# Finishing output rows: the final weight multiplied early on GpSimd, one half scaled on ScalarE, and a shorter root at the end

## The chip, the cores and the metric

The kernel runs on one core of a Trainium2 chip. The core has five engines with their own in-order instruction queues: TensorE (PE in the profile, with its weight loads as PEld), VectorE (DVE), ScalarE (ACT), GpSimd (POOL) and SyncE (SP), whose queue here only issues DMAs. The engines wait for each other through semaphores. The metric is the device time of one execution in microseconds (us), lower is better.

## The reference

The reference is one layer of a bidirectional encoder, applied to two sequences ("prompt" and "sample", 1024 tokens of 1024 features each, float32), followed by a final normalisation:

```python
def layer(x, c, ...):
    ...                                   # attention and Fourier mixing side by side
    x = x + ga1 * mix
    h2 = rmsnorm(x, g_ffn) * (1.0 + sc2) + sh2
    ffn = (jax.nn.silu(h2 @ w_gate) * (h2 @ w_up)) @ w_down
    return x + ga2 * ffn

def trunk(x, c):
    ...
    return rmsnorm(x, g_final)            # y = x / sqrt(mean(x*x) + 1e-6) * g_final, row by row
```

Only the last two lines matter here. For each output row the kernel needs `x + ga2 * ffn`, its mean of squares over 1024 features, the reciprocal root of that, and then the row times the root times the final weight `g_final`.

## The kernel before, in words

The two sequences run one after the other; `s` is 0 for the prompt and 1 for the sample. The work in front (conditioning vectors, attention, Fourier part) takes the first 750 us or so; then comes the feed-forward part of the prompt and then that of the sample, each with a gate/up stage and a down stage.

All large products are done to nearly float32 accuracy in three passes: `split` (lines 62 to 64) makes of a tile a rounded high part `wh` (a cast on ScalarE, line 63) and a remainder `wl` (a subtraction on VectorE, line 64), and `mm3` (lines 78 to 81) adds three matmuls. So every matmul operand loaded from memory costs a cast and a subtraction before TensorE can use it; there are eight buffers each for `wh` and `wl`.

The feed-forward matrices are multiplied by a scheme of Strassen's kind with seven products of half size. In the down stage `prod2` (one product) loops over `f`, 11 blocks: it loads two tiles with DMAs on SP (lines 1758 and 1759), splits them, and adds 12 matmuls into four PSUM banks, one for each group `t` of 128 rows. The products go into the bank sets X, Y and Z in a fixed order. After each block a `hook` may issue one step of other work; the steps are lists of small functions. `behind()` puts what a step issues on ScalarE and VectorE after the latest split. Beyond that, a compile-time planner decides the order of the instructions on each engine from its own estimate of when each is ready.

The output has four quarters: row half 0 or 1, and column half 0 or 1. `c11` and `u2` hold the two column halves of row half 0, `p1` and `u3` those of row half 1, each as four tiles of 128 x 512 (one for each `t`). `gf` holds the final weight, copied to all partitions.

- During the product into Z with index 4, the steps `early0` add the residual to `u2` and square-sum `c11`, which is complete.
- During the last product into Y (index 3), the steps `early1` complete `u3`, and `early2` square-sums `u3` on ScalarE (`first_squares`, with a tiny addition on POOL). In the sample, `early2` also multiplies `c11` by its half of `gf` on VectorE (line 1859).
- Then `rows_out` finishes row half 1: `last_part` completes the missing quarter (`p1`) on VectorE (lines 1788 and 139), square-sums it on ScalarE (line 1790), and calls `rstd`, a reciprocal root of six tiny POOL operations (lines 106 to 111: add, power, and a correction step of four). Two steps later `scale` multiplies both halves by root and weight in one VectorE operation each (line 1799), and one step later `store` writes both from SP (line 1805). In the prompt these steps run during the last product into Z (index 2); in the sample they run between the matmuls of the end.
- Row half 0 of the prompt is finished in the same way, but its steps are kept in `pending` and run in the first blocks of the sample's gate/up stage, behind splits.
- Row half 0 of the sample is the end of the kernel. The operands of the last product were split earlier and lie in SBUF (`held`), so it runs on TensorE row group by row group. After each group comes `last_part`, then a multiplication of `u2` by its weight (line 1878) and a scaling of `c11` and `u2` by the root on VectorE (line 1880), and two stores (line 1881).

Of the kernel before, what the change touches and what calls it, by code (L numbers as in the profile page):

```python
# [12 lines left out]
F32 = mybir.dt.float32  # L13
# [3 lines left out]
ALU = mybir.AluOpType  # L17
# [4 lines left out]
P = 128  # L22
# [31 lines left out]
def hybrid_encoder_kernel(ctx: ExitStack, tc: tile.TileContext, a: dict):  # L54
    nc = tc.nc
# [28 lines left out]
    tiny = ctx.enter_context(tc.tile_pool(name="tiny", bufs=4))  # L84
# [8 lines left out]
    mhalf = const.tile([P, 4], F32, name="mhalf")  # L93
# [3 lines left out]
    def rstd(ms, n, rest=None):  # L97

        v = tiny.tile([P, 4], F32, name="rs_v")[:, :n]
        y = tiny.tile([P, 4], F32, name="rs_y")[:, :n]  # L100
        w = tiny.tile([P, 4], F32, name="rs_w")[:, :n]
        r = tiny.tile([P, 4], F32, name="rs_r")[:, :n]
        if rest is None:
            nc.gpsimd.tensor_scalar(out=v, in0=ms, scalar1=EPS, scalar2=None, op0=ALU.add)
        else:
            nc.gpsimd.tensor_tensor(out=v, in0=ms, in1=rest, op=ALU.add)
        nc.gpsimd.tensor_tensor(out=y, in0=v, in1=mhalf[:, :n], op=ALU.pow)  # L107
        nc.gpsimd.tensor_tensor(out=w, in0=y, in1=y, op=ALU.mult)
        nc.gpsimd.tensor_tensor(out=w, in0=w, in1=v, op=ALU.mult)
        nc.gpsimd.tensor_scalar(out=w, in0=w, scalar1=-0.5, scalar2=1.5, op0=ALU.mult, op1=ALU.add)  # L110
        here["p"] = nc.gpsimd.tensor_tensor(out=r, in0=w, in1=y, op=ALU.mult).ins
        return r

    s1 = [const.tile([P, NC], F32, name=f"s1_{s}") for s in range(2)]
# [23 lines left out]
    def add(out, x, y, eng):  # L138
        eng.tensor_tensor(out=out, in0=x, in1=y, op=ALU.add)  # L139
# [27 lines left out]
    with ExitStack() as st:  # L167
        p1b = st.enter_context(ExitStack())
        w2 = p1b.enter_context(tc.tile_pool(name="p1b", bufs=1, side="right", reuse_waits="tile"))
        w = st.enter_context(tc.tile_pool(name="p1", bufs=1, reuse_waits="tile"))  # L170
        pp = st.enter_context(tc.tile_pool(name="p1_ps", bufs=8, space=PSUM, reuse_waits="tile"))

        def bank():
            return pp.tile([P, 512], F32, tag="b", name="bank")
# [281 lines left out]
        def zboth(k, between):  # L456
            eo = st1["eo", k]
            pz = [bank() for _ in range(2)]
            mz = tiny.tile([P, 4], F32, name="mz")
            if 3 < k + 2 < nk:  # L460
                norm(k + 2)
            for i in range(2):
                for c in range(NC):
                    mm3(pz[i][:, :DZ], eo[i][0][:, c, :], eo[i][1][:, c, :], wz_h[:, c, :], wz_l[:, c, :], c == 0, c == NC - 1)
                    if i == 0 and c in (1, NC - 1):
                        between(c)
            if k < 2 or k == nk - 1:
# [46 lines left out]
        def flush():  # L514
            for dst, t in st1.pop("st", ()):
                nc.sync.dma_start(dst, t)
# [288 lines left out]
        z = zboth(nk - 1, lambda c: flush() if c == 1 else None)  # L805
# [409 lines left out]
    with ExitStack() as st:  # L1215
        w = st.enter_context(tc.tile_pool(name="p3", bufs=1, side="right", reuse_waits="tile"))
# [118 lines left out]
        for k in range(nit + 4):  # L1335
# [7 lines left out]
            if k < nit:  # L1343
                s, b, h, u = items[k]
# [22 lines left out]
            m = k - 11  # L1367
# [7 lines left out]
    with ExitStack() as st:  # L1375
        w = st.enter_context(tc.tile_pool(name="p5", bufs=1, reuse_waits="tile"))
# [6 lines left out]
        def quad(tag, dt=F32):  # L1383
            return w.tile([P, 4, 512], dt, tag=tag, name=tag, bufs=1)
# [94 lines left out]
        r, wc = S.pop("rgu"), quad("H41")  # L1479
# [16 lines left out]
        r = wc = None  # L1496
# [27 lines left out]
        def val():  # L1524
            return w5.tile([P, 512], F32, tag="v", name="val", bufs=VALS)
# [10 lines left out]
        gf, first_w = None, None  # L1536
        order = [fi + half * (NF // 2) for fi in range(NF // 2) for half in range(2)]
        pending = []
        for s in range(2):
# [80 lines left out]
            for n, f in enumerate(order):  # L1620
# [51 lines left out]
                x, y, z = bank(), bank(), bank()  # L1672
# [5 lines left out]
                u2 = val()  # L1678
# [6 lines left out]
                u3 = val()  # L1685
# [18 lines left out]
            ga = w5.tile([P, D], F32, tag="ga", name="ga2", bufs=1)  # L1704
            if gf is None:
                gf = S["gf"]
# [69 lines left out]
            m, me = {}, {}  # L1776

            def first_squares(half, t, v):

                m[half, t] = tiny.tile([P, 2], F32, name=f"ms_{half}")  # L1780
                me[half, t] = tiny.tile([P, 1], F32, name=f"me_{half}")
                jk = val()
                nc.scalar.activation(jk, v, AF.Square, scale=1.0 / 32.0, accum_out=m[half, t][:, 0:1])
                nc.gpsimd.tensor_scalar(out=me[half, t], in0=m[half, t][:, 0:1], scalar1=EPS, scalar2=None, op0=ALU.add)

            def last_part(half, t, v, g, ps, z, m=m, me=me, ga=ga):

                nc.vector.tensor_tensor(out=z, in0=ps, in1=ga[:, 512 * g : 512 * g + 512], op=ALU.mult)  # L1788
                add(v, v, z, nc.vector)
                nc.scalar.activation(z, v, AF.Square, scale=1.0 / 32.0, accum_out=m[half, t][:, 1:2])  # L1790
                return rstd(m[half, t][:, 1:2], 1, me[half, t])

            def rows_out(v0, v1, half, g, ps, s=s, last_part=last_part):

                rr = {}

                def scale(t):
                    for j, v in enumerate((v0[t], v1[t])):
                        nc.vector.scalar_tensor_tensor(out=v, in0=v, scalar=rr[t][:, 0:1], in1=gf[:, 512 * j : 512 * j + 512],  # L1799
                                                       op0=ALU.mult, op1=ALU.mult)  # L1800

                def store(t):
                    r0 = 512 * half + P * t
                    for j, v in enumerate((v0[t], v1[t])):
                        nc.sync.dma_start(ys[s][r0 : r0 + P, 512 * j : 512 * j + 512], v)
                    v0[t] = v1[t] = None

                def at(i):
                    if 0 <= i - 3 < 4:
                        store(i - 3)  # L1810
                    if 0 <= i - 2 < 4:
                        scale(i - 2)
# [22 lines left out]
            u2 = [val() for _ in range(4)]  # L1835
# [3 lines left out]
            c11 = [val() for _ in range(4)]  # L1839
# [3 lines left out]
            u3 = [val() for _ in range(4)]  # L1843
            for t in range(4):
                add(u3[t], Y[t], p1[t], nc.vector)
            Z = [bank() for _ in range(4)]
# [8 lines left out]

            def early2(t):
                first_squares(1, t, u3[t])
                if s == 1:
                    nc.vector.tensor_tensor(out=c11[t], in0=c11[t], in1=gf[:, :512], op=ALU.mult)

            prod2(Z, 4, True, True, hooks([functools.partial(early0, t) for t in range(4)]
                                          + [functools.partial(resid, p1[t], t, (1, 0), None) for t in range(4)],
# [6 lines left out]
            if s == 1:  # L1869
                ext = quad("H20")  # L1870
                for t in range(4):
                    tt = slice(t * P, t * P + P)
                    for f, q in enumerate(held):
                        mm3(Z[t], q[:, 0, tt], q[:, 1, tt], q[:, 2, :], q[:, 3, :], False, f == NF // 2 - 1, True)
                        if steps and f % 3 == 2:
                            steps.pop(0)()
                    r = last_part(0, t, u2[t], 1, Z[t], ext[:, t, :])
                    nc.vector.tensor_tensor(out=u2[t], in0=u2[t], in1=gf[:, 512:], op=ALU.mult)
                    for g, v in enumerate((c11[t], u2[t])):
                        nc.vector.tensor_scalar(out=v, in0=v, scalar1=r[:, 0:1], scalar2=None, op0=ALU.mult)  # L1880
                        nc.sync.dma_start(ys[1][P * t : P * t + P, 512 * g : 512 * g + 512], v)
                break

# [118 lines left out]
```

## Time and profile before

| what | us |
|---|---|
| median of three runs | 2030.23 (2030.05 to 2032.83) |
| the profiled execution | 2031.4 |
| its span | 2029.6 |
| TensorE busy | 1981.8 |
| VectorE busy | 1391.9 |
| ScalarE busy | 890.9 |
| GpSimd busy | 828.4 |

The profiled execution's own time is 1.8 us longer than its span; all positions below are microseconds from the start of that span. A row of the time order has the start, the duration, the engine, the line, the operation, output and inputs with their shapes, and at the end in brackets how long the engine was idle before and what ended that. In a row of the time order that merges several instructions ("x2"), the duration is that of the group. A row of the grouped view has count, busy time, mean duration in ns, and idle time before. On the positions: the prompt's last product into Y begins near 1323 and its rows of half 1 are finished from 1354 to 1380; the sample's gate/up stage begins near 1385; the sample's last product into Y begins near 1960, and its last matmul ends near 2020.6.

### The profile page before, as it was taken

The page shows a single profiled execution, that of the slowest core. Times are in us where ns is not written, and L with a number is a line of the kernel's source. Part 1 is how long each engine was busy: PE and PEld are TensorE (multiplying, and loading weights), DVE is VectorE, ACT ScalarE, POOL GpSimd, SP SyncE. Part 2 cuts the span into 40 slices and gives each one's busy share as a digit, 9 for nine tenths or more (in the row PEclk, how much of TensorE's full clock was granted, in tenths as well). Part 3 has the DMA queues.
Part 4 walks back from the last instruction along what each step waited for, and adds up shares of the span by engine and source line. Part 5 has one row for each costly group of instructions (what it writes and reads, how often), then busy time and mean ns, then how long its engine had stood idle before and what let it go on. Part 6 is the DMA issues. An engine that isn't in the chain of part 4 may idle for free.

```text
span 2029.6 us, 28369 instructions
## 1 busy us (share of the span) xinstructions
PE 1981.8 (98%) x9910; PEld 1642.0 (81%) x9910; DVE 1391.9 (69%) x2076; ACT 890.9 (44%) x1732; POOL 828.4 (41%) x972
## 2 busy tenths in 40 slices
PE   7899999999999999999999999999999999999998
PEld 3788778888888878888888888877888888888876
DVE  4567758666676779677777576678755655667675
ACT  2665435555565564333333365453333333336441
POOL 0554313111313227779779410333554454410142
PEclk9999999999999999999999999999999999999999
DMA  9796884444643475645645587674322322358662
GB/s 387 257 326 202 270 324 114 130 100 91 154 125 137 144 260 178 213 164 189 211 158 192 178 306 252 212 233 170 120 99 104 108 100 104 103 189 277 221 225 96
DMA packets 183037, 376.64 MB, mean 186 GB/s; under 512 B 17997, under 2 KB 57549, under 8 KB 179053
## 3 DMA queue, kind: packets, MB, share of 16 engines
q1 hardware_dynamic: 165548, 321.33, 46.5%
q0 software_dynamic: 17344, 53.49, 8.9%
q8 instruction: 78, 1.28, 0.3%
q14 instruction: 67, 0.54, 0.1%
HBM read 262.75 MB, written 120.39 MB: 189 GB/s over the span
## 4 chain that ended last, share of the span: by engine, by line
PE 55%; DVE 3%; DMA 1%; issue 1%; POOL 1%; ACT 1%; SPq 0%; DVEq 0%; ACTq 0%; POOLq 0%
PE bank L80 19%; PE bank L79 18%; PE bank L81 18%; DVE wl L64 1%; DVE val L139 1%; DMA draw<-s_d 1%; DVE val L1799 0%; ACT wh L63 0%; DMA val<-x_d 0%; DVE val L136 0%; POOL val L139 0%; POOL rs_y L107 0%; DMA draw<-in_w_down_dram 0%; DVE val L1788 0%; DMA rgu<-in_wgu_dram 0%
## 5 line engine op out<-in xcount | busy, mean ns | idle before, releaser
L79 PE MATMUL bank<-H,wh 128*128 128x512 f32 x1232 | 480.1, 390 | 4.4 <-DVE val L1679 2.0
L80 PE MATMUL bank<-H,wh 128*128 128x512 f32 x1232 | 479.4, 389 | 0.3 <-DVE H L64 0.3
L81 PE MATMUL bank<-H,wl 128*128 128x512 f32 x1232 | 479.3, 389 | 0.2 <-DVE wl L64 0.2
L79 PEld LDWEIGHTS bank<-H,wh 128*128 128x128 f32 x1232 | 231.2, 188 | 55.5 <-DVE val L1679 3.2
L81 PEld LDWEIGHTS bank<-H,wl 128*128 128x128 f32 x1232 | 231.3, 188 | 48.5 <-DVE wl L64 0.5
L80 PEld LDWEIGHTS bank<-H,wh 128*128 128x128 f32 x1232 | 231.3, 188 | 48.1 <-DVE H L64 0.6
L64 DVE TENSOR_TENSOR wl<-draw,wh 128x512 fp32r<-128x512 f32 x286 | 201.2, 739 | 86.0 <-ACT wh L63 86.0
L139 DVE TENSOR_TENSOR val<-bank,val 128x512 f32<-128x512 f32 x200 | 136.5, 688 | 154.1 <-PE bank L81 150.6
L63 ACT CAST wh<-draw 128x512 fp32r<-128x512 f32 x286 | 168.6, 620 | 157.7 <-PE bank L80 97.9
L80 PE MATMUL bank<-wl,wh 128*128 128x512 f32 x572 | 223.8, 391 | 3.7 <-DVE wl L64 3.7
L139 POOL TENSOR_TENSOR val<-val 128x512 f32<-128x512 f32 x58 | 82.0, 1422 | 352.1 <-DVE val L1773 188.0
L81 PE MATMUL bank<-wh,wl 128*128 128x512 f32 x572 | 222.7, 389 | 0.0
L79 PE MATMUL bank<-wh 128*128 128x512 f32 x572 | 222.6, 389 | 0.0
L63 ACT CAST wh<-rgu 128x512 fp32r<-128x512 f32 x172 | 107.1, 622 | 258.7 <-PE bank L80 201.2
L63 ACT CAST wh<-val 128x512 fp32r<-128x512 f32 x133 | 82.3, 622 | 258.3 <-PE bank L80 241.7
L64 DVE TENSOR_TENSOR wl<-rgu,wh 128x512 fp32r<-128x512 f32 x172 | 169.1, 983 | 4.5 <-ACT wh L63 4.5
L64 DVE TENSOR_TENSOR wl<-val,wh 128x512 fp32r<-128x512 f32 x133 | 125.0, 941 | 67.8 <-ACT wh L63 67.7
L136 POOL TENSOR_TENSOR val<-rgu 128x512 f32<-128x512 f32 x80 | 113.0, 1413 | 94.2 <-DMA rgu<-in_wgu_dram 81.6
L80 PEld LDWEIGHTS bank<-wl,wh 128*128 128x128 f32 x572 | 107.3, 188 | 29.5 <-DVE wl L64 7.4
L79 PEld LDWEIGHTS bank<-wh 128*128 128x128 f32 x572 | 107.4, 188 | 22.5
L81 PEld LDWEIGHTS bank<-wh,wl 128*128 128x128 f32 x572 | 107.4, 188 | 21.9
L1238 DVE TENSOR_REDUCE mx<-ps_s 128x1 f32<-128x1024 f32 x64 | 78.1, 1221 | 60.1 <-PE ps_s L1233 59.9
(393 smaller groups left out, 4056.8 us busy)
## 6 DMA issues: line engine op xcount, KB each, us to landing
rgu<-in_wgu_dram SPq DMA_DIRECT2D x86, 512.0 KB, 4.4
draw<-s_d SPq DMA_DIRECT2D x143, 256.0 KB, 3.7
s_d<-val POOLq DMA_DIRECT2D x88, 256.0 KB, 4.0
draw<-t_d SPq DMA_DIRECT2D x88, 256.0 KB, 4.3
s_d<-val SPq DMA_DIRECT2D x66, 256.0 KB, 2.7
draw<-in_w_down_dram SPq DMA_DIRECT2D x55, 256.0 KB, 4.6
wada<-in_w_ada_dram SPq DMA_DIRECT2D x11, 1024.0 KB, 9.6
xt<-in_x_dram SPq DMA_DIRECT2D x16, 512.0 KB, 10.3
```

Source lines behind the costliest of these rows:

```text
L63: here["a"] = nc.scalar.copy(hi, src).ins
L64: here["v"] = (eng or nc.vector).tensor_tensor(out=lo, in0=src, in1=rd(hi), op=ALU.subtract).ins
L79: nc.tensor.matmul(out, lh, rh, start=first, stop=False, skip_group_check=cont)
L80: nc.tensor.matmul(out, lh, rl, start=False, stop=False, skip_group_check=cont)
L81: here["t"] = nc.tensor.matmul(out, ll, rh, start=False, stop=last, skip_group_check=cont).ins
L136: return eng.tensor_tensor(out=out, in0=x, in1=y, op=ALU.subtract).ins
L139: eng.tensor_tensor(out=out, in0=x, in1=y, op=ALU.add)
L1238: nc.vector.tensor_reduce(out=mx, in_=ps, axis=AX.X, op=ALU.max)
```

## The change

- In `early2`, both sequences now multiply `u3` by the second half of `gf` and `c11` by the first half, on POOL. Before, only the sample did the one for `c11`, on VectorE.
- `scale` in `rows_out` no longer multiplies the half that was complete early (`j != g`) by the weight, which it has already; it is multiplied by the root on ScalarE. The other half is still done on VectorE by root and weight in one operation.
- At the end, `last_part` is called with `end=True` and uses a new function `rstd1`: the addition and the power stay on POOL, the correction is three VectorE operations instead of four on POOL. Then `c11` is scaled on ScalarE, and `u2` on VectorE by root and weight in one operation; the multiplication of line 1878 is gone. The stores come after both.

```diff
+    def rstd1(ms, rest):
+        v, y, w, r = ...                                    # four tiny tiles as in rstd
+        nc.gpsimd.tensor_tensor(out=v, in0=ms, in1=rest, op=ALU.add)
+        nc.gpsimd.tensor_tensor(out=y, in0=v, in1=mhalf[:, :1], op=ALU.pow)
+        nc.vector.scalar_tensor_tensor(out=w, in0=y, scalar=v, in1=y, op0=ALU.mult, op1=ALU.mult)
+        nc.vector.tensor_scalar(out=w, in0=w, scalar1=-0.5, scalar2=1.5, op0=ALU.mult, op1=ALU.add)
+        nc.vector.tensor_tensor(out=r, in0=w, in1=y, op=ALU.mult)
+        return r
...
 def last_part(half, t, v, g, ps, z, m=m, me=me, ga=ga, end=False):
...
+    if end:
+        return rstd1(m[half, t][:, 1:2], me[half, t])
     return rstd(m[half, t][:, 1:2], 1, me[half, t])
...
 def scale(t):
     for j, v in enumerate((v0[t], v1[t])):
-        nc.vector.scalar_tensor_tensor(out=v, in0=v, scalar=rr[t][:, 0:1], in1=gf[:, 512 * j : 512 * j + 512],
-                                       op0=ALU.mult, op1=ALU.mult)
+        if j != g:
+            nc.scalar.mul(v, v, rr[t][:, 0:1])
+        else:
+            nc.vector.scalar_tensor_tensor(out=v, in0=v, scalar=rr[t][:, 0:1], in1=gf[:, 512 * j : 512 * j + 512],
+                                           op0=ALU.mult, op1=ALU.mult)
...
 def early2(t):
     first_squares(1, t, u3[t])
-    if s == 1:
-        nc.vector.tensor_tensor(out=c11[t], in0=c11[t], in1=gf[:, :512], op=ALU.mult)
+    nc.gpsimd.tensor_tensor(out=u3[t], in0=u3[t], in1=gf[:, 512:], op=ALU.mult)
+    nc.gpsimd.tensor_tensor(out=c11[t], in0=c11[t], in1=gf[:, :512], op=ALU.mult)
...
-    r = last_part(0, t, u2[t], 1, Z[t], ext[:, t, :])
-    nc.vector.tensor_tensor(out=u2[t], in0=u2[t], in1=gf[:, 512:], op=ALU.mult)
-    for g, v in enumerate((c11[t], u2[t])):
-        nc.vector.tensor_scalar(out=v, in0=v, scalar1=r[:, 0:1], scalar2=None, op0=ALU.mult)
+    r = last_part(0, t, u2[t], 1, Z[t], ext[:, t, :], end=True)
+    nc.scalar.mul(c11[t], c11[t], r[:, 0:1])
+    nc.vector.scalar_tensor_tensor(out=u2[t], in0=u2[t], scalar=r[:, 0:1], in1=gf[:, 512:], op0=ALU.mult, op1=ALU.mult)
+    for g, v in ((0, c11[t]), (1, u2[t])):
         nc.sync.dma_start(ys[1][P * t : P * t + P, 512 * g : 512 * g + 512], v)
```

More of the change, by code (lines that the diff above doesn't have):

```diff
@@ L111, in rstd @@
         here["p"] = nc.gpsimd.tensor_tensor(out=r, in0=w, in1=y, op=ALU.mult).ins
+        return r
+    def rstd1(ms, rest):
+        v = tiny.tile([P, 4], F32, name="rs_v")[:, :1]
+        y = tiny.tile([P, 4], F32, name="rs_y")[:, :1]
+        w = tiny.tile([P, 4], F32, name="rs_w")[:, :1]
+        r = tiny.tile([P, 4], F32, name="rs_r")[:, :1]
+        nc.gpsimd.tensor_tensor(out=v, in0=ms, in1=rest, op=ALU.add)
[3 more added lines that the diff above has]
+        nc.vector.tensor_tensor(out=r, in0=w, in1=y, op=ALU.mult)
         return r
@@ L1784, in first_squares, with last_part @@
                 nc.gpsimd.tensor_scalar(out=me[half, t], in0=m[half, t][:, 0:1], scalar1=EPS, scalar2=None, op0=ALU.add)
-            def last_part(half, t, v, g, ps, z, m=m, me=me, ga=ga):
+            def last_part(half, t, v, g, ps, z, m=m, me=me, ga=ga, end=False):
                 nc.vector.tensor_tensor(out=z, in0=ps, in1=ga[:, 512 * g : 512 * g + 512], op=ALU.mult)
```

## The prediction

> **What bounds the kernel now.** I read the page first, then the busy time of each engine by stretches, then the waits of TensorE, and last the time order of VectorE and GpSimd (POOL) around each wait.
>
> ```profile
> span 2029.6 us, 28369 instructions
> PE 1981.8 (98%) x9910; PEld 1642.0 (81%) x9910; DVE 1391.9 (69%) x2076; ACT 890.9 (44%) x1732; POOL 828.4 (41%) x972
> ```
> ```profile
> core 0: us, PE busy (x) PEld busy (x) DVE busy (x) ACT busy (x) POOL busy (x), PEclk, DMA share, GB/s
> 1350.00:1375.00 25.00, 23.12 (x101) 18.52 (x100) 20.04 (x32) 11.68 (x23) 10.22 (x24) 1.00 0.70 232
> 1400.00:1425.00 25.00, 22.89 (x99) 17.98 (x97) 24.30 (x30) 8.36 (x18) 19.81 (x26) 1.00 0.42 148
> 1450.00:1475.00 25.00, 25.00 (x112) 20.71 (x111) 15.51 (x17) 8.24 (x15) 13.96 (x13) 1.00 0.34 117
> 2000.00:2025.00 25.00, 20.64 (x92) 16.74 (x90) 13.23 (x22) 3.62 (x10) 8.80 (x29) 1.00 0.28 106
> ```
>
> TensorE is the bound: 98% busy at a granted clock of 1.00. The reader sees two kinds of stretch. In a plain one (1450) it never stops and does 112 matmuls in 25 us, so 12 of them, one block f of a product, take 2.68 us. In 1350 and 1400 it loses 1.9 and 2.1 us, and VectorE is busy 20 and 24 of 25 us. The change touches just these: the output rows of the prompt (s = 0), whose second half is finished while the sample (s = 1) begins, and the end. Here is what TensorE waits for around them:
>
> ```profile
> 1366.03 0.50 PE L80 MATMUL bank<-wl,wh 128*128 128x512 f32 x1 [0.93 <-DVE wl L64]
> 1372.72 0.50 PE L80 MATMUL bank<-wl,wh 128*128 128x512 f32 x1 [0.95 <-DVE wl L64]
> 1416.16 0.50 PE L79 MATMUL bank<-H,wh 128*128 128x512 f32 x1 [1.68 <-DVE val L1679]
> 1425.32 0.50 PE L79 MATMUL bank<-H,wh 128*128 128x512 f32 x1 [0.70 <-DVE val L139]
> 1965.62 0.50 PE L80 MATMUL bank<-wl,wh 128*128 128x512 f32 x1 [1.19 <-DVE wl L64]
> ```
>
> All end on VectorE. The first four, 4.26 us together, lie where VectorE scales rows; that and the end is all the change can win. The fifth comes before anything changed.
>
> **The rows of the prompt (1354 to 1380).** VectorE scales two halves per row; one of them goes to ScalarE.
>
> ```profile
> L1799 DVE SCALAR_TENSOR_TENSOR val<-val,rs_r,gf x24: 737/746/1777, 1359.2 to 2007.8; 128x512 f32<-128x512 f32 x24
> 1362.16 1.42 DVE L1799 SCALAR_TENSOR_TENSOR val<-val,rs_r,gf 128x512 f32<-128x512 f32 x2 [0.36 <-POOL rs_r L111]
> 1370.04 1.42 DVE L1799 SCALAR_TENSOR_TENSOR val<-val,rs_r,gf 128x512 f32<-128x512 f32 x2 [1.54 <-POOL rs_r L111]
> L792 ACT ACTIVATE wm<-wraw,cmask 128x512 fp32r<-128x512 f32 x8 | 5.4, 721 | 0.0
> ```
>
> A pair takes 1.42 us, one alone 0.75: 0.67 us saved a row. But both pairs shown started only when POOL's reciprocal root was there, so for the first wait just the row behind that root counts: 0.93 - 0.67 = 0.26 us stays. For the second wait two more rows have become shorter, and 0.95 us goes. Gain 1.62 us, unless the subtractions ahead (L64) come later, below. The price on ScalarE is 0.72 us a half, by the nearest row with a scale from memory; it is 44% busy, so I cost it at nothing. If a half stood in front of a cast that TensorE needs, it would cost its 0.72 us. The stores on SP wait for both halves and hold the loads behind them; they go with the later half, no later than now as long as ScalarE is not behind.
>
> **The start of the sample (1385 to 1426).**
>
> ```profile
> 1385.01 0.69 DVE L64 TENSOR_TENSOR wl<-rgu,wh 128x512 fp32r<-128x512 f32 x1 [3.79 <-ACT wh L63]
> 1412.30 1.40 DVE L1799 SCALAR_TENSOR_TENSOR val<-val,rs_r,gf 128x512 f32<-128x512 f32 x2
> 1416.80 0.69 DVE L64 TENSOR_TENSOR wl<-rgu,wh 128x512 fp32r<-128x512 f32 x1 [0.69 <-ACT wh L63]
> 1421.18 3.48 DVE L1799 SCALAR_TENSOR_TENSOR val<-val,rs_r,gf 128x512 f32<-128x512 f32 x2
> ```
>
> Between 1385.01 and 1416.80 no row of VectorE has an idle time in front; two scaled rows lie in it before the wait of 1.68 us. Without their ScalarE halves it is 2 x 0.67 = 1.34 us shorter: 0.34 stays. The pair at 1421.18 took 3.48 us beside POOL's work; half of that is 1.74, more than the 0.70 us wait behind it. Gain 1.34 + 0.70 = 2.04 us. After these waits TensorE is next held by nothing for 500 us.
>
> **The end.** TensorE is done near 2020.6; then a chain runs alone.
>
> ```profile
> 2022.88 0.69 DVE L1878 TENSOR_TENSOR val<-val,gf 128x512 f32<-128x512 f32 x1 [0.79 <-ACT H L1790]
> 2022.92 0.69 POOL L106 TENSOR_TENSOR rs_v<-ms,me 128x1 f32<-128x1 f32 x1 [4.33 <-ACT H L1790]
> 2023.70 0.55 POOL L107 TENSOR_TENSOR rs_y<-rs_v,mhalf 128x1 f32<-128x1 f32 x1
> 2025.15 0.19 POOL L111 TENSOR_TENSOR rs_r<-rs_w,rs_y 128x1 f32<-128x1 f32 x1
> 2025.37 0.88 DVE L1880 TENSOR_SCALAR val<-val,rs_r 128x512 f32<-128x512 f32 x2 [1.80 <-POOL rs_r L111]
> 1991.65 0.19 POOL L106 TENSOR_TENSOR rs_v<-ms,me 128x1 f32<-128x1 f32 x1 [15.51 <-ACT val L1790]
> L1244 DVE RECIPROCAL rr<-sm 128x1 f32<-128x1 f32 x64 | 10.4, 163 | 25.7 <-ACT p L1243 25.4
> ```
>
> Now: from the end of rs_y (2024.25) to VectorE's scaling (2025.37) are 1.12 us. After: three tiny VectorE operations, not shown here in this form, by the 163 ns of the nearest row and 0.04 us between them, some 0.6 us (bounds 0.3 to 1.1, where the gain would be gone). Gain 0.5. The product of L1878 now joins the scaling, so rs_v no longer runs beside it: 0.69 towards 0.19, of which I take 0.35. Against it, both halves are ready at nearly one moment (0.75 on VectorE, 0.72 on ScalarE) and SP issues their two stores one after the other; the last store leaves about 0.15 later after the root than now. Gain 0.7 us, bounds 0 to 1.2.
>
> **What it adds: products on POOL.** Eight per pass (u3 and c11 for four rows) during the product that uses Y for the last time: sixteen new on POOL, four gone from VectorE (L1859).
>
> ```profile
> L139 POOL TENSOR_TENSOR val<-val 128x512 f32<-128x512 f32 x58 | 82.0, 1422 | 352.1 <-DVE val L1773 188.0
> 1403.01 1.29 POOL L136 TENSOR_TENSOR val<-rgu 128x512 f32<-128x512 f32 x1
> 1404.38 1.62 POOL L136 TENSOR_TENSOR rgu<-rgu 128x512 f32<-128x512 f32 x1
> 1406.07 1.63 POOL L136 TENSOR_TENSOR val<-rgu 128x512 f32<-128x512 f32 x1
> 1407.78 1.62 POOL L136 TENSOR_TENSOR val<-rgu,val 128x512 f32<-128x512 f32 x1
> 1408.17 1.78 DVE L64 TENSOR_TENSOR wl<-rgu,wh 128x512 fp32r<-128x512 f32 x1
> 1411.08 0.70 DVE L64 TENSOR_TENSOR wl<-rgu,wh 128x512 fp32r<-128x512 f32 x1
> L64 DVE TENSOR_TENSOR wl<-draw,wh 128x512 fp32r<-128x512 f32 x18 | 12.9, 749 | 7.1 <-ACT wh L63 7.0
> L64 DVE TENSOR_TENSOR wl<-draw,wh 128x512 fp32r<-128x512 f32 x13 | 8.5, 684 | 1.3 <-ACT wh L63 1.3
> L1859 DVE TENSOR_TENSOR val<-val,gf 128x512 f32<-128x512 f32 x4 | 3.8, 954 | 0.0
> L1784 POOL TENSOR_SCALAR me<-ms 128x1 f32<-128x1 f32 x16 | 8.6, 538 | 51.9 <-ACT val L1783 51.3
> ```
>
> The middle rows show the price: while POOL streams such operations, one every 1.70 us, a subtraction with both inputs in SBUF takes 1.78 us and not 0.70. So a product costs VectorE up to 1.1 us. The Trainium skill, "SBUF — State Buffer", section "Who interferes with whom", says why: the two engines share a port pair that one of them holds for a whole instruction while the other is blocked. By that rule all sixteen products block VectorE fully, 17.6 us in sum; the rows above agree for a stream, and whether it reaches TensorE is the rival below.
>
> The last two L64 rows are VectorE's in the stretches concerned, 1333 to 1354 (prompt) and 1971 to 1984 (sample). In the prompt POOL would stream from about 1334: eight products and one old addition at 1.70, four small ones near 0.7, 18 us, to 1352. Between them VectorE gets one operation each, 13; TensorE takes two a block, 18 / 2.68 x 2 = 13.4. The pace nearly holds, but the 7.1 us that VectorE now idles, its lead, are eaten. I take 0.9 us of waits there, and the rows' chain starting 2.75 us later. With that the wait of 0.93 becomes 0.9 + (0.93 + 2.75 - 0.67 - 0.9) = 3.0 us in all, and the later one falls inside it. Against 0.93 + 0.95 = 1.88 now, this stretch loses 1.1 in place of winning 1.62. In the sample TensorE has no rows behind this product (its last blocks lie split in SBUF), VectorE loses 3.8 us of L1859, and only the pace counts: I take a loss of 0.6. Bounds of the two costs: from nothing (all in idle time) to 8 x 1.1 - 4.0 = 4.8 in the prompt (4.0 us of the idle comes late enough to help) and 8.8 - 3.8 = 5.0 in the sample.
>
> **Sum.** +1.1 (prompt rows) - 2.0 (sample start) + 0.6 (sample's products) - 0.7 (end) = -1.0 us. The profiled execution took 2031.4 us, 1.8 around its span and 1.2 above the median of 2030.23; from that median I get 2029.2.
>
> **The rivals.**
> - *Free products.* VectorE's idle time swallows them. For it: 7.1 us of idle, and that the planner may put products where VectorE waits for loads. Against: at 1971 the idle is 1.3 us. It gives -1.62 - 2.04 - 0.7 = -4.4: 2025.8.
> - *The products hold TensorE* (slower). The blocked subtractions pass through at their upper bounds: -4.4 + 4.8 + 5.0 = +5.4, 2035.6. For it: TensorE waits for L64 there already (1.19 us at 1965.62). It is slower from 4.4 us of cost on, by over 0.2% from 8.5.
> - *The rows gain nothing.* Scaling still waits for POOL's root, and a half on ScalarE queues behind casts that wait for TensorE:
>
> ```profile
> 1403.46 0.62 ACT L63 CAST wh<-rgu 128x512 fp32r<-128x512 f32 x1 [2.44 <-PE bank L80]
> ```
>
> A half behind such a cast is up to 2.4 us late, the store with it, and SP's loads after that. Then 2.0 and 0.7 of the gains shrink to 0.7, against costs of 0.6 and 1.1: +1.0, 2031.2. Against it: ScalarE is idle in those gaps.
>
> **How the numbers follow.** Chances: my sum 0.49 (own range 2027 to 2032), free products 0.24, products that hold TensorE 0.19, rows without gain 0.08. A measurement here tells about 0.2%, 4.1 us. The free case lies beyond that mostly and my sum's low edge nearly: faster 0.23. The holding case mostly: slower 0.18. The rest 0.59. The range leaves out the outer half of the two extreme cases: 2025.0 to 2034.0.
>
> **What would show it.** Right: in the prompt POOL rows of 1.6 us from 1334 to about 1352 with subtractions of 1.7 beside them, the L1788 of the first row some 2 to 3 us later after the start of the product, and L1799 in singles; at the sample's start no wait over 0.5 us; at the end about 8.3 us from the last matmul in place of 9.0. Wrong: if the wait near 1366 shrinks (products free), if waits of over 2 us in sum appear between blocks at 1335 to 1350 or 1971 to 1988, or if the planner puts other work into another order.

## The result, and the profile after

The changed kernel took 2037.56 us (median of 12 runs, 2034.11 to 2040.07) against 2031.83 us (2029.36 to 2037.41) of the kernel before on the same chip: a ratio of 1.0026, 95% interval 1.0018 to 1.0035, or about 5.3 us longer. Forecast were 1.0 us less, 2029.2 us, in a range of 2025.0 to 2034.0; the measured time lies above it. The profiled execution took 2034.4 us with a span of 2032.6.

From the page of the changed kernel, first the span and the busy times, then two groups (busy time, mean ns of one, idle time just before and its cause):

```profile
span 2032.6 us, 28372 instructions
PE 1980.4 (97%) x9910; PEld 1639.8 (81%) x9910; DVE 1409.2 (69%) x2064; ACT 902.2 (44%) x1748; POOL 846.9 (42%) x972
L64 DVE TENSOR_TENSOR wl<-draw,wh 128x512 fp32r<-128x512 f32 x286 | 225.8, 828 | 72.9 <-ACT wh L63 72.5
L80 PE MATMUL bank<-wl,wh 128*128 128x512 f32 x572 | 225.3, 394 | 7.4 <-DVE wl L64 7.4
```
The same two groups on the page of the kernel before:
```profile
L64 DVE TENSOR_TENSOR wl<-draw,wh 128x512 fp32r<-128x512 f32 x286 | 201.2, 739 | 86.0 <-ACT wh L63 86.0
L80 PE MATMUL bank<-wl,wh 128*128 128x512 f32 x572 | 223.8, 391 | 3.7 <-DVE wl L64 3.7
```

VectorE has 12 instructions fewer and is busy 17 us longer. The same 286 subtractions of the down stage take 24.6 us more, and TensorE waits for them 7.4 us in place of 3.7. Where? The busy time by stretches of the changed kernel (the number behind a busy time is the count of instructions, the last three columns are the granted clock, the DMA share and GB/s):

```profile
1300.00:1325.00 25.00, 22.16 (x95) 17.25 (x94) 21.19 (x21) 10.61 (x19) 12.39 (x9) 1.00 0.73 236
1340.00:1350.00 10.00, 10.00 (x46) 8.29 (x45) 7.78 (x10) 4.66 (x8) 4.11 (x4) 1.00 0.63 213
```
and of the kernel before:
```profile
1300.00:1325.00 25.00, 25.00 (x112) 20.65 (x111) 15.87 (x23) 10.39 (x19) 9.07 (x7) 1.00 0.74 261
```

TensorE loses 2.84 us in a stretch where the kernel before lost nothing and for which the prediction had no term: the product into Z with index 4. In 1340 to 1350, where the prediction had the products, POOL is busy 4.1 of 10 us.

Two profiled executions can differ by some us in parts that nothing touches: in the first 780 us, TensorE in the 12 kernels profiled beside the kernel before is between 3.7 us ahead of it and 4.0 us behind it. So I compare by stage. TensorE does its 9910 matmuls in the same order in every kernel here; a stage runs from the start of one numbered matmul to that of another, and what is shown is its length less that in the kernel before. The stages are the product into Z index 4 (Z4; 1303.5 to 1319.4 in the prompt, 1939.1 to 1953.8 in the sample), the last product into Y (Y3; to 1361.5, with the first blocks of the next, and to 1989.9), the rest of the prompt's product into Z index 2 with its rows (Z2; to 1381.3), the sample's start (to 1429.1), and the end from the last matmul on. "Order" is SP's in Z2, below. "Timed" is the ratio of the runs, in us, with its interval.

```
us           Z4 pr  Y3 pr  Z2 pr  start  Z4 sa  Y3 sa  end    sum    timed             order
changed       3.8   -0.2    3.5   -3.6    3.8   -0.7   -0.4   +6.2   +5.3 (3.7, 7.1)   new
pinned        0.0    1.7    4.1   -2.6    0.2    0.7   -0.3   +3.8   +4.5 (1.4, 7.3)   new
forced        2.7    1.1   -0.5   -3.0    3.8   -0.3   -0.3   +3.6   +3.0 (1.0, 5.3)   old
no_c11        0.8    1.1    1.6   -2.5    0.0    1.3   -0.7   +1.6   -0.2 (-2.8, 2.2)  new
tail_only     0.0    0.5   -0.4   -0.3    0.0   -0.1   -0.7   -1.0   -0.6 (-3.0, 1.8)  old
prod_only     2.7    1.5    0.2   -0.2    3.8   -1.1    0.0   +6.9   +7.1 (4.3, 9.7)   old
pinned_forced 0.0    2.1    1.6   -2.6    0.0    0.4   -0.4   +1.0   +3.0 (0.8, 5.5)   old
no_prod_forced 0.7   0.2   -1.8   -2.6    0.2    0.2   -0.7   -3.9   -2.8 (-4.7, -1.0) old
v3            0.6    1.1   -0.5   -2.5    0.8   -0.2   -0.7   -1.5   -1.2 (-3.2, 1.0)  old
memset_c11    2.3    1.0    2.0   -2.9    1.5    0.6   -0.7   +3.7   +6.3 (3.5, 8.9)   new
v5            0.0    0.1   -1.4   -2.4    0.0    0.1   -0.7   -4.2   -2.8 (-5.5, -0.4) old
v4            0.0   -0.5   -0.4   -2.8    0.0   -1.2   -0.1   -5.0   -1.2 (-3.2, 1.0)  old
```

`tail_only` touches only the end, and its other stages differ by at most 0.5. Single waits vary more: that for VectorE near 1329 (0.61 us in the kernel before), ahead of any product in Y3, is anything from nothing to 1.5 us in the others, and that near 1965 (1.19) from nothing to 1.7. So a figure under about 1.5 us for one stage counts for little unless the wait behind it is known. The row "changed" names two losses, Z4 in both passes and Z2 in the prompt, which outweigh a gain as forecast at the sample's start.

**The first loss: products where nothing held them.** POOL's time order in the changed kernel (line 1877 is the product of `c11`, 1876 that of `u3`, 152 an addition of the residual to a tile, 1797 the tiny addition of `first_squares`):

```profile
1290.73 0.37 POOL L1797 TENSOR_SCALAR me<-ms 128x1 f32<-128x1 f32 x1 [23.66 <-ACT val L1796]
1291.18 1.59 POOL L1877 TENSOR_TENSOR val<-val,gf 128x512 f32<-128x512 f32 x1
1292.73 3.44 POOL L152 TENSOR_TENSOR val<-val 128x512 f32<-128x512 f32 x2
1296.26 0.53 POOL L1797 TENSOR_SCALAR me<-ms 128x1 f32<-128x1 f32 x1
1296.87 1.61 POOL L1877 TENSOR_TENSOR val<-val,gf 128x512 f32<-128x512 f32 x1
...
1306.44 3.44 POOL L152 TENSOR_TENSOR val<-val 128x512 f32<-128x512 f32 x2
```
the same stretch of VectorE, and of TensorE:
```profile
1302.94 1.79 DVE L1786 TENSOR_TENSOR val<-val,ga 128x512 f32<-128x512 f32 x1
1304.65 2.38 DVE L64 TENSOR_TENSOR wl<-draw,wh 128x512 fp32r<-128x512 f32 x2
1306.95 1.77 DVE L1786 TENSOR_TENSOR val<-val,ga 128x512 f32<-128x512 f32 x1
```
```profile
1305.77 0.39 PE L79 MATMUL bank<-wh 128*128 128x512 f32 x1
1307.08 0.50 PE L80 MATMUL bank<-wl,wh 128*128 128x512 f32 x1 [0.92 <-DVE wl L64]
1311.09 0.50 PE L80 MATMUL bank<-wl,wh 128*128 128x512 f32 x1 [0.97 <-DVE wl L64]
1315.09 0.50 PE L80 MATMUL bank<-wl,wh 128*128 128x512 f32 x1 [0.94 <-DVE wl L64]
```

The program issues `c11`'s products in `early2`, in the next product. But `behind()` puts only ScalarE's and VectorE's steps behind a split. An instruction on POOL goes where the planner takes it to be ready, and `c11` was ready here, some 40 us ahead of the place in the program. From 1290.73 to the end of the last row POOL has no idle time for 19 us; many of VectorE's operations with two inputs in SBUF take 1.8 us and not 0.68 (a pair with one such takes 2.38), and TensorE waits three times. From start to start the matmul of 1307.08 came 1.31 us after the one before it, where 0.23 is usual: 1.1 us lost, and 3.3 at all three. In the kernel before POOL paused in this place for its loads, and VectorE caught up:

```profile
1295.22 3.09 POOL L139 TENSOR_TENSOR val<-val 128x512 f32<-128x512 f32 x2 [0.89 <-DMA val<-x_d]
1302.40 2.53 POOL L139 TENSOR_TENSOR val<-val 128x512 f32<-128x512 f32 x2 [2.87 <-DMA val<-x_d]
```

The sample repeats it, with three waits of 0.93 to 0.98 from 1946.65 to 1954.64.

**The second loss: loads behind stores.** SP's queue in the prompt's rows, before and then after (out_dram is a store of a finished half, the two kinds of `draw` are the loads of a block):

```profile
1363.98 0.46 SPq L1759 DMA_DIRECT2D draw<-in_w_down_dram  x1
1364.49 0.51 SPq L1758 DMA_DIRECT2D draw<-s_d  x1
1365.04 0.47 SPq L1759 DMA_DIRECT2D draw<-in_w_down_dram  x1
1366.67 1.00 SPq L1805 DMA_DIRECT2D out_dram<-val  x2
```
```profile
1367.63 4.09 SPq L1823 DMA_DIRECT2D out_dram<-val  x3
1371.78 0.42 SPq L1771 DMA_DIRECT2D draw<-s_d  x1
1372.30 0.40 SPq L1823 DMA_DIRECT2D out_dram<-val  x1
1372.75 0.42 SPq L1772 DMA_DIRECT2D draw<-in_w_down_dram  x1
```

Written with s and w for the two loads and O for a store, the queue around the four rows was OOsOOwswOOsOOwswsw and is now OOOsOwOOOsOwswswsw. Both stores of the third row and one of the fourth now stand ahead of the loads of block 7 (the three at 1367.63). The last of them could go only when ScalarE had scaled its half at 1370.65, which waited for POOL's root. The loads that left SP at 1364.49 and 1365.04 now leave at 1371.78 and 1372.75, and ScalarE's casts and then TensorE wait for them (1.87 us, and 0.23 for the subtraction behind that cast):

```profile
1370.65 0.72 ACT L1815 ACTIVATE val<-val,rs_r 128x512 f32<-128x512 f32 x1 [1.92 <-POOL rs_r L111]
1376.65 0.62 ACT L63 CAST wh<-draw 128x512 fp32r<-128x512 f32 x1 [0.73 <-DMA draw<-in_w_down_dram]
```
```profile
1377.32 0.50 PE L79 MATMUL bank<-wh 128*128 128x512 f32 x1 [1.87 <-ACT wh L63]
```

At the sample's start TensorE has no idle row between 1385 and 1430 any more, where 1.68 and 0.70 us stood; in the other kernels with this part of the change 0.28 to 0.65 of the first is left.

### The profile page after: what moved, and what is told of

It reads as the page before. It is cut to its first block, busy times and chain, and to the rows that moved or that the text cites. A ratio compares the mean times of both kernels' runs of the same rounds, so it can differ in the third digit from the quotient of the medians.

```text
span 2032.6 us, 28372 instructions
## 1 busy us (share of the span) xinstructions
PE 1980.4 (97%) x9910; PEld 1639.8 (81%) x9910; DVE 1409.2 (69%) x2064; ACT 902.2 (44%) x1748; POOL 846.9 (42%) x972
## 3 DMA queue, kind: packets, MB, share of 16 engines
q8 instruction: 78, 1.28, 0.3%
## 4 chain that ended last, share of the span: by engine, by line
PE 56%; DVE 3%; issue 1%; DMA 1%; POOL 1%; ACT 0%; SPq 0%; POOLq 0%; DVEq 0%; ACTq 0%
PE bank L80 19%; PE bank L81 19%; PE bank L79 19%; DVE wl L64 2%; DVE val L1786 1%; DMA draw<-t_d 0%; DVE val L152 0%; ACT wh L63 0%; DMA X<-hc_d 0%; DMA draw<-s_d 0%; DMA draw<-in_w_down_dram 0%; POOL rs_y L107 0%; DVE val L149 0%; POOL val L152 0%; DVE H L64 0%
## 5 line engine op out<-in xcount | busy, mean ns | idle before, releaser
L64 DVE TENSOR_TENSOR wl<-draw,wh 128x512 fp32r<-128x512 f32 x286 | 225.8, 828 | 72.9 <-ACT wh L63 72.5
L64 DVE TENSOR_TENSOR wl<-val,wh 128x512 fp32r<-128x512 f32 x133 | 126.7, 954 | 65.7 <-ACT wh L63 65.5
L64 DVE TENSOR_TENSOR wl<-rgu,wh 128x512 fp32r<-128x512 f32 x172 | 168.4, 979 | 3.7 <-ACT wh L63 3.6
```

What stands on the lines that cost most here:

```text
L64: here["v"] = (eng or nc.vector).tensor_tensor(out=lo, in0=src, in1=rd(hi), op=ALU.subtract).ins
```

## The experiments

The changed kernel is the base of all that follow but `tail_only` and `prod_only`, which are the kernel before with one part added.

**Moving one suspect each: `pinned` and `forced`.** `pinned` makes POOL's order follow the program:

```diff
 # first_squares
-nc.gpsimd.tensor_scalar(out=me[half, t], ...)
+here["me"] = nc.gpsimd.tensor_scalar(out=me[half, t], ...).ins
 # early2
+with tc.issue_after(here["me"]):
     nc.gpsimd.tensor_tensor(out=u3[t], ...)
     nc.gpsimd.tensor_tensor(out=c11[t], ...)
```

> All eight products of a pass are put on POOL behind the small additions of the half-1 squares, so that they run during the last product into Y and not, as in the changed kernel, partly during the product into Z with index 4. Theory A (what costs is that c11's products join the eight residual additions of the earlier product): the three waits of about 0.95 us at 1305 to 1315 and those at 1945 to 1955 are gone, 7.2 us less than the changed kernel, less up to 2 us of new waits later: -2 to 0 us against the kernel before. Theory of the prediction (eight products stream in the last product into Y and VectorE cannot keep pace): new waits of 1 to 3 us at 1335 to 1352 and at 1971 to 1990, +2 to +5 us against the kernel before.

`forced` leaves the products and ties the stores of the last three of the four rows behind those loads of blocks 6 to 8 behind which they stood in the kernel before (`pin` takes the earlier instruction first):

```diff
 # store(t)
+d = nc.sync.dma_start(ys[s][r0 : r0 + P, ...], v).ins
+if half == 1 and s == 0: S["st", t, j] = d
 # prod2, loads ds and dw of block f
+if k == 2 and s == 0 and f in (6, 7, 8):
+    for j in range(2): pin(dw if f == 7 else ds, S.pop(("st", f - 5, j)))
```

> The changed kernel, with one thing undone: in the prompt's rows of half 1 the stores of rows 1, 2 and 3 keep their places in SP's queue behind the loads of blocks 6, 7 and 8, as in the kernel before. Theory B (the loads of block 7 stand 7 us later in SP's queue, behind stores that wait for scaled rows): the wait of 1.9 us near 1377 and its neighbours go, 2 to 3.3 us less than the changed kernel, about +2 to +3 us against the kernel before. Rival (the waits near 1372 to 1378 come from ScalarE's scaling in front of the casts, or from the dip of the granted clock behind them): no change, +5 us.

`pinned` ends the loss in Z4 in both passes (0.0 and 0.2) and keeps the one in Z2 (4.1); `forced` ends that in Z2 (-0.5) and keeps Z4 (2.7 and 3.8). So the two losses are separate. In time `pinned` is at 1.0022 (1.0007 to 1.0036) and `forced` at 1.0015 (1.0005 to 1.0026): differences to the changed kernel that are small beside the intervals. `pinned` missed the -2 to 0 us of its first theory, since the moved products cost TensorE time in Y3 and Z2.

**Without one part: `no_c11` and `tail_only`.**

```diff
 # no_c11, early2
-nc.gpsimd.tensor_tensor(out=c11[t], in0=c11[t], in1=gf[:, :512], op=ALU.mult)
```

> The changed kernel without the products of c11, whose weight is thereby left out of a quarter of the output; the products of u3 stay. Theory A: 7.2 us less than the changed kernel, -2 us against the kernel before, no waits at 1305 to 1315 and 1945 to 1955. If u3's products in the last product into Y are what costs: at least +2 us.

`tail_only` has the new end (`rstd1`, `c11` on ScalarE at the end) and nothing else of the change.

> The kernel before with only the end changed: the root's correction on VectorE, c11 scaled on ScalarE and u2 on VectorE by root and weight. The chain from the last matmul to the end of the span is 0.4 to 0.7 us shorter (8.99 us before); the time is that much lower, within the noise of a run. Rival (the three VectorE operations cost as much as POOL's four): no difference in the chain.

Without `c11`'s products Z4 costs 0.8 and 0.0, so it is these eight that held TensorE there, not the eight of `u3`. The time, -0.2 us, is not the -2 us expected; Z2 still costs 1.6. With the old rows and the new end the end is 0.7 us shorter and the rest stays: 0.9997 (0.9985 to 1.0009), which the timing alone cannot tell from nothing.

**The products by themselves, and both repairs: `prod_only`, `pinned_forced`, `no_prod_forced`.** `prod_only` is the kernel before with the two POOL lines in `early2`, and the old scaling.

> The kernel before with the products on POOL alone, placed as in the changed kernel (c11's in the product into Z with index 4, u3's in the last product into Y); scaling, SP's order and the end stay as before, so that these halves are multiplied by the weight twice. Theory A + B: the product into Z costs +3.8 us in each pass, the last product into Y 0 to +1, the prompt's rows (Z with index 2) less than 1 us since SP's order is that of before, nothing is won at the sample's start: +7 to +9 us. Rival (the prompt's rows are late because the products make all splits late): +3 us or more in the prompt's rows here as well.

> The changed kernel with both causes undone: all products in the last product into Y, and SP's order as before. By stage against the kernel before: product into Z 0 in both passes, last product into Y +1.7 and +0.7, prompt's rows -0.5 to +0.5, sample's start -2.6 to -3.6, end -0.3 to -0.7. Sum -1 to -2 us. If A and B were not independent, the prompt's rows would again be +2 us or more.

`no_prod_forced` is `forced` without the two product lines.

> The changed kernel without any product on POOL (the weight of those halves is left out) and with SP's order as before: what the scaling on ScalarE and the new end give without their price. By the prediction's free case -4.4 us: prompt's rows -1.6, sample's start -2.0 to -3.5, end -0.4 to -0.7, the last product into Y of the sample -0.7 since four VectorE products are gone. If the scaling in the prompt's rows is of no use (it waits for POOL's root), that stage is within 0.5 us.

`prod_only` is as slow as the changed kernel, 1.0035 (1.0021 to 1.0048), with the loss in Z4 of both passes, and SP's order is that of the kernel before (0.2 in Z2). Over all kernels the new order stands in the four that have ScalarE's halves in the prompt's half-1 rows and no tie (the last column of the table), and they lose 1.6 to 4.1 us in Z2. The wait for ScalarE's cast of 1377.32 stands in all four, with 1.87, 1.57, 1.45 and 1.44 us, and in none of the other nine profiles. Of the eight with the old order only `pinned_forced` loses there (1.6), and there the pinned stream comes just ahead. Between pairs that differ in the order alone or nearly, it is worth 4.0 (changed less `forced`; some 1.5 of this is the dip of the clock told at the end) and 2.5 us (`pinned` less `pinned_forced`). So the new order comes with ScalarE's halves: `prod_only` has the products without them and `v5` the rest without them, both with the old order. No kernel here has these halves without a product on POOL and without a tie. That the planner moves the stores because it takes ScalarE to be ready sooner is my inference.

`pinned_forced` has the change at the places that the prediction supposed. It loses 2.05 + 1.58 = 3.6 us in the prompt, 0.4 in the sample; the -1 to -2 us expected of it were missed (+3.0 timed). `no_prod_forced` has the same without the products: -1.8 in the prompt's rows, -2.6 at the sample's start, -0.7 at the end, 0.9986 (0.9977 to 0.9995). The difference is what the products cost when placed as written: 1.9 and 3.4 us in Y3 and Z2 of these two profiles, and 5.5 us between the medians of their runs (2032.74 and 2027.29).

Not all of the 3.4 is theirs, nor is the -1.8 the work of shorter rows. Here is the first row's start in the kernel before; then, of `no_prod_forced`, that start, the scaling of the fourth row, and TensorE's wait behind it:

```profile
1353.94 1.28 DVE L1788 TENSOR_TENSOR val<-bank,ga 128x512 f32<-128x512 f32 x2
```
```profile
1352.62 1.28 DVE L1806 TENSOR_TENSOR val<-bank,ga 128x512 f32<-128x512 f32 x2
1368.92 0.75 DVE L1822 SCALAR_TENSOR_TENSOR val<-val,rs_r,gf 128x512 f32<-128x512 f32 x1 [1.81 <-POOL rs_r L113]
1370.93 0.50 PE L82 MATMUL bank<-wl,wh 128*128 128x512 f32 x1 [0.22 <-DVE wl L64]
```

From the first row's start to that matmul the kernel before takes 18.78 us (to 1372.72, shown in the prediction) and `no_prod_forced` 18.31. So it is in every profile: 18.8 to 19.1 where VectorE scales both halves, 18.3 where ScalarE scales one. The fourth row's scaling waits for POOL's root, which does not come earlier when the rows before it are shorter: 16.1 us after the first row's start before, 16.3 here. So the shorter rows are worth 0.5 us. Another 1.1 us of the -1.8 comes from rows that began that much earlier against TensorE, and `v5`, whose rows here are those of the kernel before, gains 1.4 in the same way. What brought that start forward in these two profiles is open.

The first and the last product on POOL in `pinned`, whose stream lies as the prediction had it:

```profile
1335.43 1.63 POOL L1877 TENSOR_TENSOR val<-val,gf 128x512 f32<-128x512 f32 x1
...
1350.74 1.73 POOL L1878 TENSOR_TENSOR val<-val,gf 128x512 f32<-128x512 f32 x1
```
what VectorE and TensorE do beside and behind it:
```profile
1339.23 12.09 DVE L64 TENSOR_TENSOR wl<-draw,wh 128x512 fp32r<-128x512 f32 x9
```
```profile
1366.13 0.50 PE L80 MATMUL bank<-wl,wh 128*128 128x512 f32 x1 [1.13 <-DVE wl L64]
```

**Why POOL's products cost TensorE: `memset_c11`.** Each product of `c11` becomes three fills of the same tile, which read nothing and take POOL about as long (1.69 us for three):

```diff
-nc.gpsimd.tensor_tensor(out=c11[t], in0=c11[t], in1=gf[:, :512], op=ALU.mult)
+for _ in range(3):
+    nc.gpsimd.memset(c11[t], 0.0)
```

> The changed kernel with each POOL product of c11 replaced, at the same place in POOL's queue, by three POOL fills of the same tile with zero (so that this quarter of the output is zero): POOL stays occupied for about as long (3 x 0.55 us in place of 1.3 to 1.6), but reads nothing. If the cost in the product into Z comes from POOL's reads of SBUF blocking VectorE's two-input subtractions, that stage goes from +3.8 to less than +1.0 in both passes. If it comes from POOL being occupied (the residual additions and what waits for them come late), it stays at +2.5 to +3.8.

The fills went to the same place in Z4. In the time order of POOL and of VectorE there:

```profile
1293.11 1.69 POOL L1878 MEMSET val<- 128x512 f32 x3
1294.77 3.46 POOL L152 TENSOR_TENSOR val<-val 128x512 f32<-128x512 f32 x2
```
```profile
1293.48 1.28 DVE L64 TENSOR_TENSOR wl<-draw,wh 128x512 fp32r<-128x512 f32 x2
1294.69 0.68 DVE L1786 TENSOR_TENSOR val<-val,ga 128x512 f32<-128x512 f32 x1
1295.29 3.48 DVE L64 TENSOR_TENSOR wl<-draw,wh 128x512 fp32r<-128x512 f32 x2
```

Beside fills VectorE's pair of subtractions takes 1.28 us; beside the additions that follow, which read, the next pair takes 3.48. The three waits for L64 are gone. So the slow VectorE came from POOL's operations that read. That is the Trainium skill's rule on the page "SBUF — State Buffer", section "Who interferes with whom": a VectorE instruction with two inputs in SBUF contends with a GpSimd instruction that reads SBUF, not with one that only writes; these rows agree.

But Z4 still costs 2.3 and 1.5 us, of 3.8, and the time did not fall: 1.0031 (1.0017 to 1.0044). One large wait is left, of another kind:

```profile
1317.49 0.51 PE L79 MATMUL bank<-wh 128*128 128x512 f32 x1 [1.48 <-ACT wh L63]
```
SP's own waits from 1292 to 1318 (us in total, times, longest), first in this kernel, then in the kernel before:
```profile
SPq L1785 <- POOL val L152: 10.9, 6, 3.3
```
```profile
SPq L1772 <- POOL val L139: 4.8, 4, 1.6
```

A busy POOL does its residual additions later, the next residual loads on SP wait for those buffers, and the loads of the blocks are queued behind them. In the changed kernel SP waits 6.5 us in all for these additions, nearer to the kernel before, and all three of TensorE's waits in Z4 end on VectorE, 3.3 of the 3.8 us. So what shows there is the slow VectorE; what late loads alone would cost there is not shown, only that without the products' reads 1.5 and 2.3 are left.

**A version that is faster: `v3`, `v5`, `v4`.** All three take the half-1 rows of the prompt back to VectorE or tie the stores, and put no unheld product on POOL. `v5`:

```diff
 # scale
-if j != g:
+if j != g and half == 0:
 # early2: both POOL products removed; prompt, three more steps in the product into Z index 4:
+[functools.partial(weigh, c11, 0, ts) for ts in ((0, 1), (2,), (3,))]   # c11 by gf on VectorE
 # sample, after the last split:
+with tc.issue_after(here["v"]):
+    for t in range(4): nc.vector.tensor_tensor(out=c11[t], in0=c11[t], in1=gf[:, :512], op=ALU.mult)
```

`v3` is the same but for the prompt's `c11`, which POOL multiplies in `early2`, pinned as above. `v4` is `v5` with the prompt's half-1 rows split as in the change, `u3`'s products on VectorE in the last product into Y, and the stores tied as in `forced`.

> A version meant to be faster than both: the prompt's c11 products stay on POOL but behind the small additions in the last product into Y; the sample's c11 products go to VectorE behind its last split; u3 has no product and the rows of half 1 are scaled on VectorE as before (SP's order is then that of before); rows of half 0 and the end as in the change. By stage: product into Z 0, last product into Y of the prompt 0 to +1, of the sample -0.7, prompt's rows 0, sample's start -2.6 to -3.6, end -0.3 to -0.7. Sum -3 to -4.5 us. If the sample's start won its 3 us only because the prompt was late before it, that stage is 0 here.

> A version without any product on POOL: c11's products run on VectorE, in the prompt as three extra steps after the eighth step of the product into Z (where VectorE has 5 us of idle time), in the sample behind the last split; rows of half 1 are scaled on VectorE as before; rows of half 0 and the end as in the change. By stage: product into Z 0 to +0.7, last product into Y 0, prompt's rows 0, sample's start -2.5 to -3.5, end -0.4 to -0.7. Sum -2.5 to -4. If the extra steps cost their 2.4 us there, the product into Z or the last one into Y is +1.5 to +2.4.

> v5 and in addition u3's products on VectorE as three extra steps after the eighth step of the prompt's last product into Y, the prompt's rows of half 1 scaled on both engines, and SP's order as before. Prompt's rows -1 to -1.8 in place of 0, the rest as v5. Sum -3.5 to -5.5. If the extra steps take away the lead of the splits there, the last product into Y and the rows together gain nothing over v5.

`v5` took 2027.57 us against 2030.97: 0.9986 (0.9973 to 0.9998), faster than both kernels. Less the 1.4 of Z2 told above, its sum of stages, -4.2, agrees with the -2.8 that was timed. `v3` came out at 0.9994 (0.9984 to 1.0005), -1.2 us where -3 to -4.5 were expected. `v4` has the best sum of stages, -5.0, but the same time as `v3`, 0.9994 (0.9984 to 1.0005), where -3.5 to -5.5 us were expected. Of its -5.0 some 1.4 are the waits near 1329 and 1965, which are 0.2 us each in its profile. In Y3 and Z2 of the prompt together it gains nothing over `v5` (-0.9 and -1.2), as its expectation's other case had it. The rest of the miss stays open. In `v5` the stretch of the first loss is as full for TensorE as before the change, with the four products of `c11` on VectorE (1313.1 to 1320.1):

```profile
1300.00:1325.00 25.00, 25.00 (x112) 20.60 (x111) 19.31 (x26) 9.50 (x18) 10.76 (x9) 1.00 0.78 255
```

## Why the prediction was wrong

- **Where the products go.** The step "In the prompt POOL would stream from about 1334: eight products and one old addition" failed. Four of the eight, those of `c11`, streamed between 1291 and 1306, in a stage that the prediction put at nothing, and cost 3.8 us there; the sample did likewise. The place was read from the program's order, and nothing but readiness held POOL to a place. The text ahead of the prediction says that `behind()` orders ScalarE and VectorE and that the planner does the rest, but the prediction took the planner only as a way to a better place.
- **The stores.** "They go with the later half, no later than now as long as ScalarE is not behind" failed too. It looked at when one store can go, not at what stands behind it once the order changes. ScalarE scaled each half as soon as POOL's root was there (0.72 us a half, as forecast); the stores moved ahead of two loads and held them for 7 us. TensorE's wait for them, with the small one behind it, cost 2.1 to 2.5 us in each of the four kernels with the new order, and the changed kernel's Z2 lost 3.5 in all.
- **The size of the stream where it was expected.** The mechanism was right: in `pinned` POOL streams from 1335 to 1352, the lead of VectorE is eaten (nine subtractions in 12.09 us), and the large waits come afterwards, in the rows. Two terms of the forecast of +1.1 were too favourable, as `pinned_forced` shows. The waits beside the stream were 0.95 us, where 0.9 was taken. But the rows began 3.75 us later, not 2.75 (at 1362.5, of which 4.8 lay ahead of the stream, against 1353.9), and the shorter rows gave back 0.5, not 1.62: 3.3 in place of 1.1. The rest of the 3.6 is mostly the wait near 1329, ahead of the first product. In the sample Y3 lost 0.4 and 0.7 against 0.6.
- **The shorter rows.** "For the second wait two more rows have become shorter, and 0.95 us goes" failed. The -1.8 us of `no_prod_forced` in Z2 is near the -1.62 of the forecast, but by luck: the shorter rows are worth 0.5, as worked out above. The second wait is not gone: 0.1 us for ScalarE's cast, which stands behind a scaled half (0.2 in the other kernels with these halves), and 0.22 for the subtraction are left of 0.95. So a half on ScalarE, costed at nothing, does stand in front of a cast that TensorE needs.
- **The sample's start.** -2.4 to -3.6 against -2.04. Right, and somewhat low: the wait of 0.70 us is gone in all kernels with this part, and of the 1.68 us 0.28 to 0.65 are left where 0.34 was forecast (nothing in the changed kernel).
- **The end.** -0.4 in the changed kernel, -0.7 in six and -0.1 to -0.4 in four of the other ten with the new end, against -0.7. From the last matmul to the last store's leaving SP, all eleven are 0.7 us shorter; what differs lies behind that. The time order of the end of the changed kernel shows the step as forecast, with 0.22, 0.15 and 0.16 us for the three tiny operations for which 163 ns each was taken:

```profile
2027.20 0.22 DVE L122 SCALAR_TENSOR_TENSOR rs_w<-rs_y,rs_v 128x1 f32<-128x1 f32 x1 [1.69 <-POOL rs_y L121]
2027.46 0.15 DVE L123 TENSOR_SCALAR rs_w<-rs_w 128x1 f32<-128x1 f32 x1
2027.64 0.16 DVE L124 TENSOR_TENSOR rs_r<-rs_w,rs_y 128x1 f32<-128x1 f32 x1
```

- **The rivals.** The free case, -4.4 us, came to -2.8 (-4.7 to -1.0) in `no_prod_forced`, which leaves the products out. The slower rival, products that hold TensorE, had the right sign and the right mechanism (subtractions blocked by POOL) at the wrong place; that its 5.4 us resembles the 5.3 measured is chance, since Z2's loss is none of it. The third rival, rows without gain, was right that scaling still waits for POOL's root, and that is why the rows gave 0.5 us; it also had late stores delay SP's loads, but by a late half on ScalarE and not by a new order. "The planner puts other work into another order" stood among the things that would make the prediction wrong, without a price. The stores' loss is of just this kind, and that of `c11`'s products is the same planner placing the new work itself.

## What to carry to other kernels

Before a step is costed at the place where the program has it, ask what holds it there: an instruction on an engine that nothing orders goes where its inputs are ready, and a store whose producer changes its engine may change its place in a queue together with all loads behind it. An elementwise product moved from VectorE to POOL isn't free because POOL is idle: it slows VectorE's operations on two inputs while it reads, and it can make late what POOL already does for others. Four products on VectorE in a stretch where it had 9 of 25 us idle cost TensorE nothing, and four on POOL in the same stretch cost 2.7 to 3.8 us. Where several rows are finished one after the other, shortening one engine's step gains only what the slowest chain, here POOL's root, leaves.

## What the runs showed of the hardware that was not expected

- Fills on POOL leave VectorE at its pace (0.68 us) where products and additions bring it to 1.8 us.
- In the profile of the changed kernel the granted clock fell just behind the wait at 1377.32; in none of the other 12 does it fall between 300 us and the last matmul. The busy time by stretches, and two rows of TensorE:

```profile
1378.00:1383.00 5.00, 4.95 (x15) 3.91 (x16) 3.98 (x6) 3.61 (x6) 0.00 (x0) 0.66 0.66 209
```
```profile
1379.34 0.63 PE L79 MATMUL bank<-wh 128*128 128x512 f32 x1
1379.77 0.63 PE L80 MATMUL bank<-wl,wh 128*128 128x512 f32 x1
```

  Some eight matmuls came 0.43 us apart and not 0.23, about 1.5 us of the 3.5 in Z2 in that one execution. `pinned` and `no_c11` lose 4.1 and 1.6 in the same stage at a granted clock of 1.00, so the dip isn't needed for the loss; what brought it is open.
